# Delta rule of a hybrid layer on one core: inverse, solution, outputs and norms for two heads at once, with the projections in another order

## The chip, the cores and the metric

One core of one Trainium2 chip runs the whole program. The metric is device time in microseconds (us). An engine runs its own instructions in order; the five that matter here are called PE (TensorE's products), PEld (its loads of stationary operands, which run beside the products), DVE (VectorE), ACT (ScalarE) and POOL (GpSimd). SP issues the loads of the weights.

## The reference, cut to what matters

A sequence of 256 tokens with 1024 channels passes through two blocks. The first (two layers of attention and feed-forward) is not touched. The second is a hybrid layer: eight heads of a gated delta rule and four of a retention read the same projections, are gated and summed, and a feed-forward follows.

```
def chunk_gated_delta_rule(q, k, v, beta, g):       # 8 heads, d_k 128, d_v 256, chunks of 64 tokens
    ...
    lower = jnp.where(strict, jnp.einsum('bhncd,bhnmd->bhncm', k_beta, k) * decay, 0.0)
    t_inv = lax.linalg.triangular_solve(lower, eye, left_side=True, lower=True, unit_diagonal=True)
    u = jnp.einsum('bhncm,bhnme->bhnce', t_inv, v * beta[..., None])
    w = jnp.einsum('bhncm,bhnmd->bhncd', t_inv, k_beta * jnp.exp(g_cum)[..., None])
    attn = jnp.where(causal, jnp.einsum('bhncd,bhnmd->bhncm', q, k) * decay, 0.0)
    ...                                             # a scan over the chunks with a state
...
qkv = jax.nn.silu(causal_depthwise_conv(jnp.concatenate([qa, ka, va], axis=-1), conv_a))
oa = chunk_gated_delta_rule(qa, ka, va, beta, g)
oa = rmsnorm_2(oa, norm_a) * jax.nn.silu(za)
```

The kernel solves the same triangular system in two blocks of 128 tokens for each head: it inverts each 128x128 unit triangular block, solves the first, carries it over to the second, solves that, and multiplies by the masked q k matrix.

## The kernel before, in words

**Main work and pieces.** All large products run as three products of a high and a low part in fp32r (`hi`, `lo` for the weights, `XH`/`XL` or `OH`/`OL` for the activations). The weights come in chunks of 1024 rows by 256 columns; a chunk is four pieces, and a piece of the kind met here is 12 products with a 128x128 stationary operand and 256 columns. DVE and ACT split each weight into `hi` (line 188) and `lo` (line 197) ahead of its use.

**Side work, a step at a time.** All else is written as generators. The emission loop (lines 1600 to 1612) issues one piece of products, then lets each active generator run up to its next `yield`, in the order in which they were started, and then issues loads and splits of weights to come. So the order on every engine is fixed when the program is built: a `yield` puts one piece of main products between two steps, and PE stands still only where the next instruction in its order isn't ready.

**A head of the delta rule** (`delta_task`, line 1046) takes q and k from the chunk `wqka`, convolves them (`conv_silu`), and nine pieces later forms the two product groups k k and q k (line 1064, four products). DVE then makes the norms (1069 to 1075), scales with decay and beta into `nLT` and `AT` (1076, 1078), puts the small diagonal blocks in place (1082) and transposes them (1083). Then come twelve steps of an inverse that doubles its blocks (1088 to 1139): in each step a group of small products (32x32 up to s = 5, 64x64 at s = 6) and a copy by ACT (`X`) or by DVE (`DD`, `DT`) that the next step's products need. After it come three products of 256 columns with pauses between them (1146, 1150, 1155: the solution in `z` and `w`), the outputs (1164, 1165), sums for the norm (1176), a power by POOL (1179), and the scaling and split into `OH`, `OL`. A product of plain fp32 is two instructions on PE.

**The order of the chunks** is q and k of head h, v of h, the gate z of h; so heads follow each other every 12 pieces, and steps of three heads fall between the same pieces. Tiles that live over several steps are held in rings (`RING`, line 261); a task that finds its ring full runs the other generators until a place is free.

**Banks.** Main products write to two banks `w` in turn (`wbank`, line 278; two of four banks `d` while results wait for a norm's factors), side work to two banks `s` and the four `d`. The gate's chunk of head 0 asks for a bank `d` by name (line 1225).

Of the kernel before, what the change touches and what calls it, by code (L numbers as in the profile page):

```python
# [30 lines left out]
# steps that side work lets pass before it needs what others make for it  # L31
# [34 lines left out]
def body(ctx: ExitStack, tc: tile.TileContext, a):  # L66
# [42 lines left out]
    # the gains first, then x; what is needed later comes behind the first weights  # L109
# [98 lines left out]
    def ahead(i):  # L208
        """what may be loaded and split once the products of piece i are issued"""
# [50 lines left out]
    # tiles that are held over steps: no more of them than the ring has  # L260
    RING = {"y": 2, "qk": 3, "qn": 2, "v": 4, "zg": 4, "DD": 3, "nLT": 3, "AT": 3, "z": 2}

    def hold(shape, tag):
# [3 lines left out]
        if tag == "z":  # L267
            zn[0] += 1
            return REG[:, 3072 + 512 * (zn[0] % 2):3584 + 512 * (zn[0] % 2)].rearrange("p (a b) -> p a b", a=2)
        return TW(shape, tag, RING[tag])  # L270

    zn = [0]
# [15 lines left out]
    wn = [0]  # L288
# [23 lines left out]
    def products(todo, xl_last=False):  # L312
        """(out, hi, lo, xh, xl, first, last): what was split last comes last"""
# [33 lines left out]
    def N_chunk(src, xs, n, post):  # L347
        """n < 128 columns in a piece"""
# [41 lines left out]
    def D_tail(grp, src, n, ops, post, pre=None):  # L390
        """the last two chunks, a bank after the other"""
# [18 lines left out]
    def W_pair(src, xs, posts):  # L410
        """two chunks of outputs at once, over the tiles of x"""
# [23 lines left out]
    def X_pair(src, xs, posts):  # L435
        """512 columns, a bank for each half of the tokens"""
# [29 lines left out]
    def split(src, hi, lo):  # L466
        """the second part a step after the first"""
# [25 lines left out]
    def sum_ch(out, parts):  # L493
        """sums over the channels, a token per partition; 32 tokens at a time, as the weights' load is what they take"""
# [19 lines left out]
    def renorm():  # L514
        """the splits of x * g * r, for the chunks after the first"""
# [73 lines left out]
    # over the keys of two blocks, for the queries of the second: all of the first, or with the window  # L589
# [4 lines left out]
    # key > query: column > partition  # L594
# [16 lines left out]
    def attend(q, k, v, slot, window=False, sink=None, delay=0, done=False):  # L611
        """q, k: [128, T], a head on each half of the partitions; v(t, half) -> [128, 64]"""
# [38 lines left out]
        for h in range(2):  # L651
# [3 lines left out]
            # blocks: (q0, k0), (q1, k0), (q1, k1)  # L655
# [11 lines left out]
    # ================= the first block =================  # L667
# [7 lines left out]
    def feed_x(b, g, xs, norm, norm2=None, g2=None, first=False):  # L675
        """after xT's pair b is complete: x * g and its splits, the squares"""
# [31 lines left out]
    # attention of layer 0  # L708
# [59 lines left out]
    def tables():  # L768
        """of the second block"""
# [9 lines left out]
    # feed-forward with a short convolution  # L779
# [63 lines left out]
    # attention of layer 1  # L843
# [45 lines left out]
    # ================= between the blocks =================  # L889
# [7 lines left out]
    def stat2():  # L897
# [4 lines left out]
        # r1 = 1 / sqrt(mean x^2 + eps), and r1 r2 with r2 the factor of x g r1  # L902
# [23 lines left out]
    # ================= the second block =================  # L926
# [10 lines left out]
    def decay_task(bank):  # L937
        # beta and g, a token per partition
# [63 lines left out]
    def conv4(src, u, y, base):  # L1002
        """src, u, y: [128, 2, T]; tiles base[i] of conv_a"""
# [37 lines left out]
    # the small blocks on the diagonal, and the transposes of the inverses  # L1041
    BLOCKS = [slice(o, o + 32) for o in range(0, 128, 32)]
    FULL = [(T1([128, 2, 128], name="DT%d" % i), T1([64, 2, 64], name="DF%d" % i)) for i in range(3)]
    ident32 = T1([128, 32], name="ident32")

    def delta_task(h, bank):
# [3 lines left out]
        q, k = qk[:, 0], qk[:, 1]  # L1050
        sq = TW([128, 512], "sq")[:, :T]
        S.activation(sq, q, AF.Square)
        # the norms of k go into beta and v, those of q into the norm behind
        tk, bk, nbk = (TW([128, 2], n, 1) for n in ("tk", "bk", "nbk"))
        qe, kv = (TW([128, 2], n, 3) for n in ("qe", "kv"))
        # the inverse, block by block of twice the size: D (0) and its transpose (1)
        DD = hold([128, 2, 2, 32], "DD")
        DT, DF = FULL[h % 3]
        V.tensor_copy(DD[:, 1], bc(ident32, 2))
        nLT, AT = hold([128, 384], "nLT"), hold([128, 384], "AT")  # L1060
        nd = nLT.rearrange("p (b c) -> p b c", b=3)[:, 0:3:2]
        for x, out, b in ((k, nLT, nbk), (q, AT, bk)):
# [24 lines left out]
        V.tensor_scalar(qe, p[:, 0:2], 128.0 * EPS, 128.0 * EPS * EPS, op0=OP.mult, op1=OP.add)  # L1087
        for s in range(1, 7):
            yield
            p = PT()  # L1090
            pv = p[:, :128].rearrange("p (b c) -> p b c", b=2)
            pd = p[:, :64].rearrange("p (b c) -> p b c", b=2)
            X = TW([128, 2, 64], "X")
            Xd = X.rearrange("p b c -> p (b c)")[:, :64].rearrange("p (b c) -> p b c", b=2)
            if s < 5:
                for o in BLOCKS:
                    for b in range(2):
                        mm(pd[o, b], nd[o, b, o], DD[o, 0, b], True, True)
                cp("S", Xd, pd)
            elif s == 5:  # L1100
                for o in (0, 64):
                    for b in range(2):
                        mm(pd[o + 32:o + 64, b], nd[o:o + 32, b, o + 32:o + 64], DD[o:o + 32, 0, b], True, True)
                for o in (32, 96):
                    cp("S", Xd[o:o + 32], pd[o:o + 32])
            else:
                for b in range(2):
                    mm(pv[64:128, b], nd[0:64, b, 64:128], DF[:, b], True, True)
# [3 lines left out]
            pv = p[:, :128].rearrange("p (b c) -> p b c", b=2)  # L1112
            pd = p[:, :64].rearrange("p (b c) -> p b c", b=2)
            if s < 5:
                for o in BLOCKS:
                    for b in range(2):
                        mm(pd[o, b], DD[o, 1, b], Xd[o, b], True, True)
            elif s == 5:
                for o in (32, 96):
                    for b in range(2):  # L1120
                        mm(pd[o:o + 32, b], DT[o:o + 32, b, o:o + 32], Xd[o:o + 32, b], True, True)
            else:
                for b in range(2):
                    mm(pv[0:64, b], X[64:128, b], DT[64:128, b, 64:128], True, True)
            if s < 5:
                V.copy_predicated(DD[:, 0], bc(lvl[:, s], 2), pd)
# [7 lines left out]
            elif s == 5:  # L1134
                V.tensor_copy(DF[32:64, :, 0:32], pd[32:64])
                V.transpose(DT[0:32, :, 32:64], pd[32:64])
                V.transpose(DT[64:96, :, 96:128], pd[96:128])
            else:
                V.tensor_copy(DT[0:64, :, 64:128], pv[0:64])
        while h not in vt:  # L1140
            yield
        v = vt.pop(h)
        z = hold([128, 2, 256], "z")
# [6 lines left out]
        mm(p[:, :256], nLT[:, 128:256], z[:, 0], True, True)  # L1150
        w = TW([128, 256], "e")
        V.tensor_tensor(w, v[:, 1], p[:, :256], op=OP.add)
        yield
        p = PT()
        mm(p[:, :256], DT[:, 1], w, True, True)
        cp("S", z[:, 1], p[:, :256])
        free("v", "DD", "nLT")
        while h not in sz:
            yield
        yield  # L1160
        p = PT()
        for e in range(2):
            c = slice(e * 128, e * 128 + 128)
            mm(p[:, e * T:e * T + T], z[:, 0, c], AT[:, 0:256], True, False)
            mm(p[:, e * T + 128:e * T + T], z[:, 1, c], AT[:, 256:384], False, True)
        free("z", "AT")
        sq = square(p)
        zg = sz.pop(h)
        for e in range(2):
            if e:  # L1170
# [599 lines left out]
```

## Time and profile before

| what | value |
|---|---|
| three runs | 1344.65, 1344.09, 1341.1 us (median 1344.09) |
| span of the profiled execution | 1341.2 us (its time beyond the span is not listed) |
| PE busy | 1317.4 us, 98% |
| PEld, DVE, ACT, POOL busy | 93%, 73%, 55%, 2% |
| instructions on PE | 11824 |
| granted TensorE clock | 0.995 of full speed over the span |
| HBM read | 212.86 MB, 159 GB/s |

The stage of the delta rule lies between about 605 and 876 us of the span. A busy PE is not PE at its peak; what a group of instructions costs PE is read from the start of its first load of a stationary operand to the start of the next group's first load.

### The profile page before, as it was taken

The page shows a single profiled execution, that of the slowest core. Times are in us where ns is not written, and L with a number is a line of the kernel's source. Part 1 is how long each engine was busy: PE and PEld are TensorE (multiplying, and loading weights), DVE is VectorE, ACT ScalarE, POOL GpSimd, SP SyncE. Part 2 cuts the span into 40 slices and gives each one's busy share as a digit, 9 for nine tenths or more (in the row PEclk, how much of TensorE's full clock was granted, in tenths as well). Part 3 has the DMA queues.
Part 4 walks back from the last instruction along what each step waited for, and adds up shares of the span by engine and source line. Part 5 has one row for each costly group of instructions (what it writes and reads, how often), then busy time and mean ns, then how long its engine had stood idle before and what let it go on. Part 6 is the DMA issues. An engine that isn't in the chain of part 4 may idle for free.

```text
span 1341.2 us, 29103 instructions
## 1 busy us (share of the span) xinstructions
PE 1317.4 (98%) x11824; PEld 1250.3 (93%) x11824; DVE 984.4 (73%) x2225; ACT 731.6 (55%) x1202; POOL 27.2 (2%) x38
## 2 busy tenths in 40 slices
PE   7999999999999999999999999999999999999998
PEld 6999999998889999999888888999999999999996
DVE  6997887778878877788778888666557556855554
ACT  6665765555765655566545544444343445655553
POOL 0000000000000000000000000000000000000000
PEclk9999999998999999999999999999999999999999
DMA  7435565554334655544333333445455564465652
GB/s 240 156 127 183 175 205 188 186 181 142 107 117 156 215 189 189 185 133 158 115 107 114 110 126 104 134 157 191 150 179 168 173 196 153 160 219 184 189 183 89
DMA packets 60470, 215.79 MB, mean 161 GB/s; under 512 B 6832, under 2 KB 7600, under 8 KB 60336
## 3 DMA queue, kind: packets, MB, share of 16 engines
q1 hardware_dynamic: 59328, 212.31, 49.1%
q8 instruction: 93, 1.52, 0.5%
q10 hardware_dynamic: 1008, 1.63, 0.4%
q14 instruction: 41, 0.34, 0.1%
HBM read 212.86 MB, written 1.05 MB: 159 GB/s over the span
## 4 chain that ended last, share of the span: by engine, by line
PE 92%; DVE 4%; ACT 2%; issue 1%; DMA 1%; POOL 0%; SPq 0%; POOLq 0%; DVEq 0%; ACTq 0%
PE ps_w L134 54%; PE ps_d L134 33%; PE ps_s L134 4%; PE ps_s L145 1%; ACT h L634 1%; DVE lo L197 1%; PE ps_d L145 1%; DMA xT<-in_x 0%; DMA raw<-in_wv0p 0%; DVE y L794 0%; ACT hi L188 0%; DVE XL L464 0%; DVE h L626 0%; DVE y L1369 0%; DVE DD L1082 0%
## 5 line engine op out<-in xcount | busy, mean ns | idle before, releaser
L197 DVE TENSOR_TENSOR lo<-raw,hi 128x512 fp32r<-128x512 f32 x801 | 519.7, 684 | 93.5 <-ACT hi L188 92.7
L188 ACT ACTIVATE hi<-raw 128x1024 fp32r<-128x1024 f32 (+1 forms) x403 | 418.1, 1046 | 168.9 <-PE ps_w L134 85.7
L134 PE MATMUL ps_w<-XH,hi 128*128 128x256 f32 x976 | 168.3, 295 | 2.5 <-ACT XH L1454 1.4
L134 PE MATMUL ps_w<-XL,hi 128*128 128x256 f32 x976 | 156.3, 283 | 0.0
L134 PE MATMUL ps_w<-XH,lo 128*128 128x256 f32 x976 | 156.1, 282 | 0.0
L134 PE MATMUL ps_w<-OH,hi 128*128 128x256 f32 x896 | 144.8, 284 | 0.0
L134 PE MATMUL ps_w<-OH,lo 128*128 128x256 f32 x896 | 142.9, 282 | 0.3 <-DVE lo L197 0.3
L134 PE MATMUL ps_w<-OL,hi 128*128 128x256 f32 x896 | 142.5, 281 | 0.0
L134 PEld LDWEIGHTS ps_w<-XH,hi 128*128 128x128 f32 x976 | 134.4, 191 | 7.8 <-ACT XH L1454 1.7
L134 PEld LDWEIGHTS ps_w<-XL,hi 128*128 128x128 f32 x976 | 133.8, 190 | 0.0
L134 PEld LDWEIGHTS ps_w<-XH,lo 128*128 128x128 f32 x976 | 133.6, 190 | 0.0
L134 PE MATMUL ps_d<-OH,hi 128*128 128x256 f32 x776 | 126.0, 283 | 0.0
L134 PEld LDWEIGHTS ps_w<-OH,hi 128*128 128x128 f32 x896 | 121.5, 188 | 3.6 <-issue 3.5
L134 PE MATMUL ps_d<-OL,hi 128*128 128x256 f32 x776 | 124.4, 281 | 0.0
L134 PE MATMUL ps_d<-OH,lo 128*128 128x256 f32 x776 | 124.3, 281 | 0.0
L134 PEld LDWEIGHTS ps_w<-OH,lo 128*128 128x128 f32 x896 | 122.1, 189 | 0.5 <-DVE lo L197 0.5
L134 PEld LDWEIGHTS ps_w<-OL,hi 128*128 128x128 f32 x896 | 121.7, 188 | 0.0
L134 PEld LDWEIGHTS ps_d<-OH,hi 128*128 128x128 f32 x776 | 104.9, 188 | 1.9 <-issue 1.7
L134 PEld LDWEIGHTS ps_d<-OL,hi 128*128 128x128 f32 x776 | 105.1, 187 | 0.3 <-DVE OL L470 0.2
L134 PEld LDWEIGHTS ps_d<-OH,lo 128*128 128x128 f32 x776 | 105.1, 188 | 0.2
L790 ACT ACTIVATE y<-u,prm 128x256 f32<-128x256 f32 x88 | 48.0, 595 | 62.4 <-DVE u L764 62.4
L764 DVE TENSOR_TENSOR u<-ps_w,RB 128x512 f32<-128x512 f32 x44 | 30.1, 689 | 63.0 <-PE ps_w L134 56.8
(378 smaller groups left out, 1644.7 us busy)
## 6 DMA issues: line engine op xcount, KB each, us to landing
raw<-in_wu SPq DMA_DIRECT2D x108, 512.0 KB, 4.2
raw<-in_wd SPq DMA_DIRECT2D x68, 512.0 KB, 3.9
raw<-in_wgb SPq DMA_DIRECT2D x24, 512.0 KB, 3.7
raw<-in_wqk SPq DMA_DIRECT2D x16, 512.0 KB, 4.0
raw<-in_wza SPq DMA_DIRECT2D x16, 512.0 KB, 3.8
raw<-in_wqkb SPq DMA_DIRECT2D x16, 512.0 KB, 4.1
raw<-in_wbra SPq DMA_DIRECT2D x16, 512.0 KB, 4.2
raw<-in_wbrb SPq DMA_DIRECT2D x16, 512.0 KB, 4.7
```

The source lines that it names most:

```text
L134: PE.matmul(out, lhsT, rhs, start=start, stop=stop, skip_group_check=True)
L145: PE.transpose(out, in_, ident)
L188: S.activation(hi[:, :w], raws[n][:, :w], AF.Copy)
L197: V.tensor_tensor(lo[:, c], raws[n][:, c], hi[:, c].bitcast(F32), op=OP.subtract)
L634: S.activation(e[h][:, c], e[h][:, c], AF.Exp, bias=nm[:, i:i + 1], accum_out=sums[:, i:i + 1])
L764: V.tensor_tensor(u, v2(bank), bc(RB, 2), op=OP.mult)
L790: S.activation(y[:, i], u[:, i], AF.Identity, bias=P_(cb, t), scale=P_(cw, 3 * t + 2))
```

## The change

Two heads form a pair. Each head still has its own convolution, its own k k and q k groups, and its own rows of `nLT` and `AT`. From there `pair_task`, which the second head of the pair enters, does the transposes, all twelve steps of the inverse, the solution and the norm for both heads: tiles have a dimension for the head, a step issues the products of both heads one behind the other, and one copy serves both. The products are the same in number and shape. The outputs of the two heads come in two steps, one behind the other. The chunks of a pair now come in the order q k (even head), z (even), q k (odd), v (even), z (odd), v (odd); the first pair starts with q k and v of head 0 together, as before. `wbank` no longer counts: it gives `w` while fewer than two results wait for a norm, else `d`, with room for six that wait; the gate of head 0 takes its bank from it. The rings of `DD`, `nLT` and `AT` hold two pairs, that of `z` one. A group of `d` chunks first lets waiting results go. Comments go, and the reserve for descriptors of dynamic transfers is set to 1024.

```
-    RING = {"y": 2, "qk": 3, "qn": 2, "v": 4, "zg": 4, "DD": 3, "nLT": 3, "AT": 3, "z": 2}
+    RING = {"y": 2, "qk": 3, "qn": 2, "v": 4, "zg": 4, "DD": 2, "nLT": 2, "AT": 2, "z": 1}
...
     def wbank(more=0):
-        if len(deferred) >= 4:
+        if len(deferred) + more >= 6:
             drain(cur["stat"])
-            late(1)
-        wn[0] += 1
-        if len(deferred) + more >= 2 and wn[0] % 4 in (3, 0):
-            return PT("d")
-        return PT("w")
+            late()
+        return PT("w" if len(deferred) + more < 2 else "d")
...
             if c == 0:
                 if s == 0:
+                    if deferred:
+                        drain(cur["stat"])
+                        late()
...
     def delta_task(h, bank):
...
+        q, k, i = qk[:, 0], qk[:, 1], h % 2
+        if i == 0:
+            P = pairs[h // 2] = Pair()
+            P.DD = hold([128, 2, 4, 32], "DD")
+            P.nLT, P.AT = hold([128, 2, 384], "nLT"), hold([128, 2, 384], "AT")
+            P.DT, P.DF = FULL[h // 2 % 2]
...
-        for x, out, b in ((k, nLT, nbk), (q, AT, bk)):
+        for x, out, b in ((k, P.nLT[:, i], nbk), (q, P.AT[:, i], bk)):
...
             if x is k:
                 for o in BLOCKS:
-                    V.copy_predicated(DD[o, 1], bc(lvl[o, 0], 2), nd[o, :, o])
-                V.transpose(DD[:, 0], DD[:, 1])
+                    V.copy_predicated(P.DD[o, 1, 2 * i:2 * i + 2], bc(lvl[o, 0], 2), nd[o, :, o])
         free("qk")
+        if i:
+            yield from pair_task(h // 2, P)
+
+    def pair_task(n, P):
+        DD, DT, DF, nLT, AT = P.DD, P.DT, P.DF, P.nLT, P.AT
+        heads = (2 * n, 2 * n + 1)
+        V.transpose(DD[:, 0], DD[:, 1])
         p = PT()
-        sum_ch(p, [sq])
+        for i in range(2):
+            sum_ch(p[:, 2 * i:2 * i + 2], [P.sq[:, i]])
...
         for s in range(1, 7):
             yield
...
                 for o in BLOCKS:
-                    for b in range(2):
-                        mm(pd[o, b], nd[o, b, o], DD[o, 0, b], True, True)
+                    for g in range(4):
+                        mm(pd[o, g], nd(g)[o, o], DD[o, 0, g], True, True)
                 cp("S", Xd, pd)
...
             yield
...
-                V.copy_predicated(DD[:, 0], bc(lvl[:, s], 2), pd)
+                V.copy_predicated(DD[:, 0], bc(lvl[:, s], 4), pd)
                 if s < 4:
                     V.transpose(DD[:, 1], DD[:, 0])
...
-        mm(p[:, :256], DT[:, 0], v[:, 0], True, True)
-        cp("S", z[:, 0], p[:, :256])
+        for i in range(2):
+            mm(p[:, i * T:i * T + T], DT[:, 2 * i], v[i][:, 0], True, True)
+        cp("S", z[:, :, 0], v2(p))
...
-            W_chunk(a["wva"][h - 1], xs0, va_post(h))
-        W_chunk(a["wza"][h], xs0, z_post(h), None, "d" if h == 0 else None)
+        if h % 2 == 0:
+            W_chunk(a["wza"][h], xs0, z_post(h))
+        else:
+            if h > 1:
+                W_chunk(a["wva"][h - 2], xs0, va_post(h - 1))
+            W_chunk(a["wza"][h], xs0, z_post(h))
+            W_chunk(a["wva"][h - 1], xs0, va_post(h))
...
-    nc = bacc.Bacc("TRN2", target_bir_lowering=False, num_devices=1)
+    nc = bacc.Bacc("TRN2", target_bir_lowering=False, num_devices=1, dynamic_dma_scratch_size=1024)
```

## Rows read from the trace of the kernel before

**Rows 1.** The page: span, and busy time of the engines.
```profile
span 1341.2 us, 29103 instructions
PE 1317.4 (98%) x11824; PEld 1250.3 (93%) x11824; DVE 984.4 (73%) x2225; ACT 731.6 (55%) x1202; POOL 27.2 (2%) x38
```
**Rows 2.** Windows: one period of a head (length, then busy time by engine).
```profile
749.15:777.28 28.13, 28.09 (x358) 24.95 (x357) 22.76 (x67) 14.21 (x29) 1.77 (x2) 1.00 0.37 114
```
**Rows 3.** Chain that ended last: start, length, what; a feed-forward stage, a norm's sums.
```profile
461.67 11.36 PE ps_w L134 x96
...
600.71 1.63 PE ps_s L134 x96
```
**Rows 4.** Timeline of PEld in the same period: start, busy time, operation, tiles, count.
```profile
749.86 0.27 PEld L134 LDWEIGHTS ps_s<-DD,nLT 32*32 32x32 f32 x16 [0.41 <-PE ps_d L134]
750.17 0.54 PEld L134 LDWEIGHTS ps_w<-XH,hi 128*128 128x128 f32 x4
...
751.78 0.24 PEld L134 LDWEIGHTS ps_d<-X,DD 32*32 32x32 f32 x16
752.06 0.53 PEld L134 LDWEIGHTS ps_w<-XH,hi 128*128 128x128 f32 x4
...
753.47 0.30 PEld L134 LDWEIGHTS ps_d<-REG,nLT 128*128 128x128 f32 x2
754.11 0.24 PEld L134 LDWEIGHTS ps_d<-DD,nLT 32*32 32x32 f32 x16 [0.33 <-DVE lo L197]
...
758.50 1.40 PEld L134 LDWEIGHTS ps_d<-AT,REG 128*128 128x128 f32 x8
760.02 0.23 PEld L134 LDWEIGHTS ps_d<-DD,nLT 32*32 32x32 f32 x16
...
767.82 0.21 PEld L134 LDWEIGHTS ps_d<-DD,nLT 32*32 32x32 f32 x8
768.07 0.54 PEld L134 LDWEIGHTS ps_w<-XH,hi 128*128 128x128 f32 x4
...
771.55 0.30 PEld L134 LDWEIGHTS ps_d<-DF,nLT 64*64 64x64 f32 x4
771.92 0.54 PEld L134 LDWEIGHTS ps_w<-XH,hi 128*128 128x128 f32 x4
...
773.90 0.73 PEld L134 LDWEIGHTS ps_d<-qk 128*128 128x128 f32 x4
...
775.41 0.22 PEld L134 LDWEIGHTS ps_d<-ones,sq 128*32 128x32 f32 x16
775.64 0.53 PEld L134 LDWEIGHTS ps_w<-XH,hi 128*128 128x128 f32 x4
```
**Rows 5.** Timeline of PEld behind the last head, where no inverse runs.
```profile
864.52 0.31 PEld L134 LDWEIGHTS ps_d<-REG,nLT 128*128 128x128 f32 x2
864.85 0.64 PEld L134 LDWEIGHTS ps_w<-XH,hi 128*128 128x128 f32 x4
...
866.36 0.31 PEld L134 LDWEIGHTS ps_d<-e,DT 128*128 128x128 f32 x2
```
**Rows 6.** Timeline of DVE behind the k k and q k groups at 773.90.
```profile
776.65 0.94 DVE L1082 COPY_PREDICATED DD<-lvl,nLT 32x64 f32<-32x64 uint8 x4
777.63 0.24 DVE L1083 STREAM_TRANSPOSE DD<-DD 128x64 f32<-128x64 f32 x1
777.80 0.44 DVE L1076 SCALAR_TENSOR_TENSOR AT<-ps_s,bk,REG 128x256 f32<-128x256 f32 x1
778.16 0.34 DVE L1078 SCALAR_TENSOR_TENSOR AT<-ps_s,bk,REG 128x128 f32<-128x128 f32 x1
```
**Rows 7.** Timeline of DVE behind the small products at 751.78.
```profile
752.94 0.22 DVE L1126 COPY_PREDICATED DD<-lvl,ps_d 128x64 f32<-128x64 uint8 x1
```
**Rows 8.** Timeline where the gate's chunk of head 0 starts.
```profile
622.33 0.73 PE L134 MATMUL ps_d<-XH,hi 128*128 128x256 f32 x4
...
623.41 1.28 DVE L764 TENSOR_TENSOR u<-ps_w,RB 128x512 f32<-128x512 f32 x2
```

More of the change, by code (lines that the diff above doesn't have):

```diff
@@ L1042, in body @@
     BLOCKS = [slice(o, o + 32) for o in range(0, 128, 32)]
-    FULL = [(T1([128, 2, 128], name="DT%d" % i), T1([64, 2, 64], name="DF%d" % i)) for i in range(3)]
+    FULL = [(T1([128, 4, 128], name="DT%d" % i), T1([64, 4, 64], name="DF%d" % i)) for i in range(2)]
     ident32 = T1([128, 32], name="ident32")
+    class Pair:
+        pass
+    pairs = {}
     def delta_task(h, bank):
@@ L1049, in delta_task @@
         yield from pause(2)
-        q, k = qk[:, 0], qk[:, 1]
-        sq = TW([128, 512], "sq")[:, :T]
-        S.activation(sq, q, AF.Square)
-        tk, bk, nbk = (TW([128, 2], n, 1) for n in ("tk", "bk", "nbk"))
[L1055 to L1061, printed above, removed]
-        for x, out, b in ((k, nLT, nbk), (q, AT, bk)):
+        q, k, i = qk[:, 0], qk[:, 1], h % 2
[4 more added lines that the diff above has]
+            P.DT, P.DF = FULL[h // 2 % 2]
+            P.sq, P.qe = TW([128, 2, T], "sqq", 1), TW([128, 4], "qe", 2)
+            V.tensor_copy(P.DD[:, 1], bc(ident32, 4))
+        P = pairs[h // 2]
+        S.activation(P.sq[:, i], q, AF.Square)
+        tk, bk, nbk = (TW([128, 2], n, 1) for n in ("tk", "bk", "nbk"))
+        kv = TW([128, 2], "kv", 4)
+        nd = P.nLT[:, i].rearrange("p (b c) -> p b c", b=3)[:, 0:3:2]
+        for x, out, b in ((k, P.nLT[:, i], nbk), (q, P.AT[:, i], bk)):
             p = PT()
@@ L1101, in delta_task @@
                 for o in (0, 64):
-                    for b in range(2):
-                        mm(pd[o + 32:o + 64, b], nd[o:o + 32, b, o + 32:o + 64], DD[o:o + 32, 0, b], True, True)
+                    for g in range(4):
+                        mm(pd[o + 32:o + 64, g], nd(g)[o:o + 32, o + 32:o + 64], DD[o:o + 32, 0, g], True, True)
                 for o in (32, 96):
@@ L1106, in delta_task @@
             else:
-                for b in range(2):
-                    mm(pv[64:128, b], nd[0:64, b, 64:128], DF[:, b], True, True)
+                for g in range(4):
+                    mm(pv[64:128, g], nd(g)[0:64, 64:128], DF[:, g], True, True)
                 cp("S", X[64:128], pv[64:128])
@@ L1111, in delta_task @@
             p = PT()
-            pv = p[:, :128].rearrange("p (b c) -> p b c", b=2)
-            pd = p[:, :64].rearrange("p (b c) -> p b c", b=2)
+            pv = p[:, :256].rearrange("p (b c) -> p b c", b=4)
+            pd = p[:, :128].rearrange("p (b c) -> p b c", b=4)
             if s < 5:
                 for o in BLOCKS:
[L1116 to L1125, printed above, removed]
-                V.copy_predicated(DD[:, 0], bc(lvl[:, s], 2), pd)
+                    for g in range(4):
+                        mm(pd[o, g], DD[o, 1, g], Xd[o, g], True, True)
+                V.copy_predicated(DD[:, 0], bc(lvl[:, s], 4), pd)
                 if s < 4:
@@ L1134, in delta_task @@
             elif s == 5:
+                for o in (32, 96):
+                    for g in range(4):
+                        mm(pd[o:o + 32, g], DT[o:o + 32, g, o:o + 32], Xd[o:o + 32, g], True, True)
                 V.tensor_copy(DF[32:64, :, 0:32], pd[32:64])
@@ L1138, in delta_task @@
             else:
+                for g in range(4):
+                    mm(pv[0:64, g], X[64:128, g], DT[64:128, g, 64:128], True, True)
                 V.tensor_copy(DT[0:64, :, 64:128], pv[0:64])
-        while h not in vt:
+        while any(h not in vt for h in heads):
             yield
-        v = vt.pop(h)
-        z = hold([128, 2, 256], "z")
+        v = [vt.pop(h) for h in heads]
+        z = hold([128, 2, 2, 256], "z")
         yield
         p = PT()
-        mm(p[:, :256], DT[:, 0], v[:, 0], True, True)
@@ L1147, in delta_task @@
-        cp("S", z[:, 0], p[:, :256])
+        for i in range(2):
+            mm(p[:, i * T:i * T + T], DT[:, 2 * i], v[i][:, 0], True, True)
+        cp("S", z[:, :, 0], v2(p))
         yield from pause(2)
         p = PT()
-        mm(p[:, :256], nLT[:, 128:256], z[:, 0], True, True)
-        w = TW([128, 256], "e")
-        V.tensor_tensor(w, v[:, 1], p[:, :256], op=OP.add)
+        w = TW([128, 2, T], "w", 1)
+        for i in range(2):
+            mm(p[:, i * T:i * T + T], nLT[:, i, 128:256], z[:, i, 0], True, True)
+            V.tensor_tensor(w[:, i], v[i][:, 1], p[:, i * T:i * T + T], op=OP.add)
@@ L1153, in delta_task @@
         yield
         p = PT()
[L1155 to L1158, printed above, removed]
-            yield
[L1160 to L1165, printed above, removed]
-        free("z", "AT")
-        sq = square(p)
@@ L1168, in delta_task @@
-        zg = sz.pop(h)
-        for e in range(2):
-            if e:
-                V.tensor_tensor(sq[:, :T], sq[:, :T], sq[:, T:], op=OP.add)
-            V.scalar_tensor_tensor(zg[:, e], p[:, e * T:e * T + T], P_("norm_a", e), zg[:, e],
-                                   op0=OP.mult, op1=OP.mult)
+        for i in range(2):
+            mm(p[:, i * T:i * T + T], DT[:, 2 * i + 1], w[:, i], True, True)
+        cp("S", z[:, :, 1], v2(p))
+        free("v", "v", "DD", "nLT")
+        while any(h not in sz for h in heads):
+            yield
@@ new lines, in pair_task @@
+        zg, sqs = [sz.pop(h) for h in heads], []
+        for i in range(2):
+            yield
+            p = PT()
+            for e in range(2):
+                c = slice(e * 128, e * 128 + 128)
+                mm(p[:, e * T:e * T + T], z[:, i, 0, c], AT[:, i, 0:256], True, False)
+                mm(p[:, e * T + 128:e * T + T], z[:, i, 1, c], AT[:, i, 256:384], False, True)
+            sq = square(p)
+            sqs.append(sq)
+            for e in range(2):
+                if e:
+                    V.tensor_tensor(sq[:, :T], sq[:, :T], sq[:, T:], op=OP.add)
+                V.scalar_tensor_tensor(zg[i][:, e], p[:, e * T:e * T + T], P_("norm_a", e), zg[i][:, e],
+                                       op0=OP.mult, op1=OP.mult)
@@ L1174, in delta_task @@
+        free("z", "AT")
         yield from pause(2)
         p = PT()
-        sum_ch(p, [sq[:, :T]])
-        tok, rt = TW([128, 2], "tok2", 4), TW([128, 2], "rt2", 4)
-        V.scalar_tensor_tensor(tok[:, :2], p[:, :2], 1.0 / 256, qe, op0=OP.mult, op1=OP.add)
-        G.tensor_tensor(rt[:, :2], tok[:, :2], mhalf[:, :2], op=OP.pow)
+        for i in range(2):
+            sum_ch(p[:, 2 * i:2 * i + 2], [sqs[i][:, :T]])
+        tok, rt = TW([128, 4], "tok4", 2), TW([128, 4], "rt4", 2)
+        V.scalar_tensor_tensor(tok, p[:, :4], 1.0 / 256, P.qe, op0=OP.mult, op1=OP.add)
@@ L1180, in delta_task @@
+        G.tensor_tensor(rt, tok, mhalf[:, :4], op=OP.pow)
         yield from pause(6)
         p = PT()
-        rows(rt, 2, p)
-        V.tensor_tensor(zg, zg, bc(p[:, :T], 2), op=OP.mult)
-        yield
-        yield from split(zg, OH[:, 2 * h:2 * h + 2], OL[:, 2 * h:2 * h + 2])
-        free("zg")
+        rows(rt, 4, p)
+        for i in range(2):
+            V.tensor_tensor(zg[i], zg[i], bc(p[:, i * T:i * T + T], 2), op=OP.mult)
+        for i, h in enumerate(heads):
+            yield
+            yield from split(zg[i], OH[:, 2 * h:2 * h + 2], OL[:, 2 * h:2 * h + 2])
+            free("zg")
```

17 lines of the change are left out of this document (8 added, 9 removed).

## The prediction

> **What bounds the kernel now.** I read the page first: PE is busy for 1317.4 of 1341.2 us, no other engine for more than three quarters [rows 1]. A busy PE says little by itself, so the question for the stage of the delta rule is what PE is busy with. The windows view gives one period of a head: 28.13 us, in which PE is never idle and DVE works for 22.76 us, 81% [rows 2]. The period holds 12 pieces of main products. What a piece costs by itself is read in the chain, in a feed-forward stage: 96 products in 11.36 us, so 12 in 1.42 us [rows 3]. 12 pieces are 17.04 us; the other 11.1 us of each period are side work on PE, in PE's own order. The change can give time back only out of these 11.1 us, or lose it by new waits of PE.
>
> The timeline of PEld shows where they go, group by group, start to start [rows 4]. A group of 16 small products takes 0.28 us (751.78 to 752.06), one of 8 0.25 us (767.82 to 768.07), four of 64x64 0.37 us (771.55 to 771.92). Beside that, a change of shape costs by itself: the piece ahead of a small group takes 1.61 us (750.17 to 751.78) and not 1.42, so 0.19 for letting the full-size products run out. A product of 256 columns in front of a small group takes 0.64 us (753.47 to 754.11), while behind the last head, where a piece follows, it takes 0.33 us (864.52 to 864.85) and delays the next piece by 0.09 us (864.85 to 866.36 is 1.51) [rows 5]. So side work is dear by its number of groups and changes of shape more than by its products.
>
> **The change part by part.** All prices are per pair, two periods of 28.13 us now, 24 pieces before and after.
>
> The joined inverse. Now: twice 8 groups of 16, 2 of 8 and 2 of 64x64, 2 x (8 x 0.28 + 2 x 0.25 + 2 x 0.37) = 6.96 us. After: 8 groups of 32, 2 of 16, 2 of eight 64x64. What the further products of a group cost no row shows directly. Below: 8 to 16 products cost 0.03 us more, 4 ns each [rows 4]. Above: 96 sums with 32 columns take 1.63 us, 17 ns each [rows 3]. Four products in a row will now use the same corner of the array, where the 8 to 16 step only filled other corners, so I go nearer to the upper end: 12 ns, 0.19 us for 16, 0.10 for 8. For four more of 64x64 I take 0.22 us, between 0.05 (four at 12 ns) and another 0.37. Sum after: 8 x 0.47 + 2 x 0.35 + 2 x 0.59 = 5.64 us. Gain 1.32 us (from -0.1 with 17 ns and 0.37, to 2.6 with 4 ns and 0.05).
>
> The Trainium skill (TensorE: Matmul & The Clock Gate, section "Wait — 56ns, not 53.3ns?") states that starts of matmuls never follow closer than about 25 ns, however small. By it 16 more would cost 0.40 us, and the joined inverse 8 x 0.68 + 2 x 0.45 + 2 x 0.59 = 7.5 us, more than now. The row speaks against it: 16 in 0.28 us is 17.5 ns each with the change of shape in it.
>
> Changes of shape. Now eight pieces of a period stand in front of small groups (seven of the inverse, one of the norm's sums): 16 x 0.19 = 3.04 us per pair. After, by the counts of yields, the inverse has twelve pieces of 24 in front of it and the norm one: 13 x 0.19 = 2.47 us. Gain 0.57 us.
>
> The products around it. Six products of 256 columns per pair stand in front of small groups now: 6 x 0.64 = 3.84 us. After, the second head enters the pair nine pieces behind its chunk, at piece 21 of the 24; the inverse takes pieces 22 to 33, which is 9 of the next pair; the solution falls on 11, 13 and 14, the outputs on 15 and 16, the sums on 18. So no inverse runs beside them: 6 x 0.33 + 2 x 0.09 = 2.16 us. The outputs (1.52 us, 758.50 to 760.02, an inverse step behind them [rows 4]) lose the same 0.19: gain 0.38. Together 2.06 us. The k k and q k groups, transposes, sums and rows of factors stay as they are in number; I cost them at nothing.
>
> The new wait at the join. Now DVE transposes the blocks (777.63, 0.24 us) before it makes `AT` [rows 6]. After, the transposes stand in `pair_task`, behind both `AT` instructions, and the inverse's first products wait for them. From the start of k k at 773.90 [rows 4] DVE ends the block copies at 777.59, +3.69; `AT` takes 0.70 (777.80 to 778.50); the transposes of twice the width take 0.31 (between 0.24 and 0.49); 0.1 to hand over: +4.80. PE has by then k k and q k with one head's sums (773.90 to 775.64, 1.74), the other head's sums 0.23, and a piece, 1.61: +3.58. Nothing else stands there in the new order, where now the rows and the first product of the solution of the head before do. PE waits 1.2 us per pair, and behind it all main products, since they are in PE's queue. If DVE comes late, as at 752.94, 1.16 us behind the start of a group that takes 0.28 [rows 7], the wait is 2.1; it can't be under 1.1, as `AT` stays.
>
> The gate's chunk of head 0. It has a bank of its own now and starts at 622.33; the bank that it would get by the new `wbank` is that of q k of head 0, which DVE reads until 623.41 + 0.64 = 624.05 [rows 8]. PE waits 1.7 us, once (nothing, if DVE came earlier). Elsewhere `wbank` gives what it gave: where two results wait, the old count had fallen on `d` as well.
>
> Order, rings, other engines. By the yields a gate tile of a pair is free at piece 52 of its count and the chunk that needs the place ends at 56, so the ring of four `zg` holds; v, y and q k rings have a place over too. The weights only change their order in SP's queue, with the same bytes. DVE and ACT save short instructions (of 45.5 us of DVE per pair [rows 2] some 3, an estimate: half of about 26 like the transposes of 0.24 [rows 6]); as neither bounds the stage I cost that at nothing, and it matters only if the cover goes: DVE would then have 42 us of work in some 53. Reserve and `d` groups: nothing, no results wait there.
>
> **Sum.** Per pair 1.32 + 0.57 + 2.06 - 1.2 = 2.75 us, four pairs 11.0, less 1.7 at the gate: 9.3 us. The last head's three products already stand free [rows 5], which takes 0.9 off, and the first heads' own waits of today give about as much back; I leave both out. The span goes from 1341.2 to 1331.9 us. The runs shown have a median of 1344.09, 2.9 above that span; a run after it should take 1344.09 - 9.3 = 1334.8 us. Own range: all low ends (wait 2.1, inverse at -0.1) leave 0 us, but both together are unlikely, so 1340; high ends (4 ns, no wait at the gate) 15 us, 1329.
>
> **The rivals.** *Groups add up.* If a product of a joined group costs as much as one does now, shape and all (17.5 ns in a group of 16), the twelve joined groups cost the old 6.96 us and only the changes of shape and the free products are saved: 9.3 - 4 x 1.32 = 4.0 us, 1340.1. For it: four in a row on one corner; against: 8 to 16 costs 0.03 us. The Trainium skill's 25 ns (the section above) would take another 4 x 0.5 us off, 1342.
>
> *No wait at the join.* If a step of another head falls in the gap, the 1.2 us are covered: 14.1 us, 1330.0. Against it: the counts of yields leave pieces 21 and 22 without other work.
>
> *DVE sets the pace of the inverse (slower).* Each step's products need a copy or transposes that DVE does behind the products of the step before. Now other heads' work lies between many of these; after, a step is a piece and a group, 1.61 + 0.47 = 2.08 us. DVE needs about 0.44 us until it sees a group, 0.6 for a wide copy and transposes, 0.1 and the longer group 0.2: some 1.35, so 0.7 us are spare, about one split of weights. At 752.94 DVE was 0.7 us late already [rows 7]. It turns the result once 24 such steps wait over 0.39 us each on the mean, that is, once DVE is late by 1.1 us throughout; with two splits in front of each, waits of 0.7 us, 24 x 0.7 = 16.8 us are lost: 1344.09 + 7.5 = 1351.6. Against it: 81% load now, and less work in it after.
>
> *It does not come about.* If tasks run into full rings, the generators run without pieces between them and PE waits for chains instead; some 9 us of it leave no change, 1344.
>
> **How the numbers follow.** What a measurement of this kernel can tell from no change is about 0.3%, 4.0 us: the runs lie 3.6 us apart. Chances: my forecast 0.60, groups add 0.12, no wait 0.08, DVE 0.09, no effect 0.11. Faster than 1340.1: nearly all of the first, half of the second, the third: 0.71. Within 0.3%: the rest of these and the last: 0.20. Slower: 0.09. The range from 1328 to 1343 holds the first three and a part of the last.
>
> **What would show it right or wrong.** Right: a pair's window of some 53.5 us where two heads take 56.3; groups of 32 small products at about 0.47 us; products of the solution with pieces on both sides at 0.33; a wait of PE of about 1.2 us for the transposes, four times; one of about 1.7 us near 622. Wrong: groups of 32 at 0.56 or more; gaps in front of most steps of the inverse with DVE named; bursts of side work without pieces, at the gate chunks above all.

## The result, and the profile after

| | before | after |
|---|---|---|
| runs, us (median) | 1341.1 to 1344.65 (1343.77), five | 1348.74 to 1357.03 (1351.24), five |
| span of the profiled execution, us | 1341.2 | 1355.2 (its time 1356.98) |
| its granted clock | 0.995 | 0.989 |

The ratio is 1.0069, with an interval of 1.0045 to 1.0093: the change costs some 7.5 us. The forecast was 1334.8 and its range ended at 1343; both were wrong, and so was the sign.

The page of after answers to [rows 1]:

```profile
span 1355.2 us, 28944 instructions
PE 1322.8 (98%) x11824; PEld 1265.1 (93%) x11824; DVE 975.2 (72%) x2149; ACT 724.7 (53%) x1158; POOL 25.2 (2%) x32
```

PE issues exactly as many products as before, and DVE and ACT have less to do. PEld is busy 14.8 us longer with the same 11824 loads: the products have become dearer, not more (a part of it lies in the stretches at a lower clock, below). The timeline of PEld, in the first pair's inverse and solution, shows which ones (to be read against [rows 4] and [rows 5]):

```profile
660.49 0.78 PEld L134 LDWEIGHTS ps_d<-DD,nLT 32*32 32x32 f32 x32 [1.39 <-DVE DD L1093]
661.31 0.54 PEld L134 LDWEIGHTS ps_w<-XH,hi 128*128 128x128 f32 x4
...
665.37 0.78 PEld L134 LDWEIGHTS ps_d<-DD,nLT 32*32 32x32 f32 x32
666.20 0.53 PEld L134 LDWEIGHTS ps_w<-XH,hi 128*128 128x128 f32 x4
...
667.81 0.78 PEld L134 LDWEIGHTS ps_s<-X,DD 32*32 32x32 f32 x32
...
680.38 0.48 PEld L134 LDWEIGHTS ps_s<-DD,nLT 32*32 32x32 f32 x16
680.90 0.54 PEld L134 LDWEIGHTS ps_w<-XH,hi 128*128 128x128 f32 x4
...
684.63 0.54 PEld L134 LDWEIGHTS ps_d<-DF,nLT 64*64 64x64 f32 x8
685.24 0.54 PEld L134 LDWEIGHTS ps_w<-XH,hi 128*128 128x128 f32 x4
...
690.18 0.74 PEld L134 LDWEIGHTS ps_s<-v,DT 128*128 128x128 f32 x4
690.94 0.64 PEld L134 LDWEIGHTS ps_w<-XH,hi 128*128 128x128 f32 x4
...
693.88 0.31 PEld L134 LDWEIGHTS ps_d<-REG,nLT 128*128 128x128 f32 x2
695.66 0.30 PEld L134 LDWEIGHTS ps_d<-REG,nLT 128*128 128x128 f32 x2 [1.47 <-DVE w L1164]
695.99 0.65 PEld L134 LDWEIGHTS ps_w<-XH,hi 128*128 128x128 f32 x4
```

A group of 32 takes 0.82 us, start to start (660.49 to 661.31; 0.83 from 665.37 to 666.20), where two groups of 16 took 2 x 0.28. At `s == 5` 16 products over two corners take 0.52 (680.38 to 680.90), where 16 over four corners took 0.28 before. The eight of 64x64 take 0.61. `v,DT` is four records in 0.76, as cheap as forecast. The first block step's `REG,nLT`, though, needs 2.11 us (693.88 to 695.99), because the second head's product starts 1.47 us late.

The chain of waits, PE alone, 600 to 900 us of after: engine, tile and line that waited, what it waited for, us in total, times, longest.

```profile
PE ps_d L134 <- DVE DD L1093: 5.3, 4, 1.4
PE ps_d L134 <- DVE w L1164: 2.6, 4, 1.1
PE ps_w L134 <- ACT hi L188: 1.7, 1, 1.7
```

The first is the forecast wait at the join, the third stands at 621, where the forecast put the gate's bank. The second was in no part of the forecast.

DVE at the join of the second pair answers to [rows 6]: the block copies (L1085), both `AT` instructions (L1079, L1081), then the transposes of `pair_task` (L1093), which end at 712.00; PE's group starts at 712.11.

```profile
710.07 0.93 DVE L1085 COPY_PREDICATED DD<-lvl,nLT 32x64 f32<-32x64 uint8 x4
711.04 0.48 DVE L1079 SCALAR_TENSOR_TENSOR AT<-ps_d,bk,REG 128x256 f32<-128x256 f32 x1
711.44 0.34 DVE L1081 SCALAR_TENSOR_TENSOR AT<-ps_d,bk,REG 128x128 f32<-128x128 f32 x1
711.70 0.30 DVE L1093 STREAM_TRANSPOSE DD<-DD 128x128 f32<-128x128 f32 x1
```

Last, three windows of after: the period of a pair (from one group of `ones,sqq` to the next), and two stretches in which the granted clock was the lower level, 1.2 GHz. Columns as in [rows 2]; the third number from the end is the clock.

```profile
770.47:830.90 60.43, 58.54 (x713) 54.66 (x713) 43.29 (x115) 26.45 (x47) 2.71 (x3) 0.94 0.33 108
714.12:724.36 10.24, 10.24 (x125) 9.44 (x123) 1.79 (x4) 3.11 (x6) 0.00 (x0) 0.50 0.33 104
775.56:782.39 6.83, 6.83 (x70) 6.21 (x71) 1.85 (x5) 0.98 (x2) 0.00 (x0) 0.50 0.48 154
```

The pair takes 60.43 us, 6.83 of them at 1.2 GHz; two heads took 56.26 [rows 2]. Before each of the two stretches PE had stood at the join and had then run a group of 0.82 us. The profile of before has no such stretch in this stage. The five runs of after fall into two kinds: spans of 1355.2 at a clock of 0.989 twice, 1347.0 to 1348.4 at 0.995 to 0.996 three times. The loss of clock costs the first kind some 7 us, an estimate from the two kinds of span; the others are still slower than before without it.

### The profile page after: what moved, and what is told of

Its sections match the earlier page's. It is cut to its first block, busy times and chain, and to the rows that moved or that the text cites. A ratio compares the mean times of both kernels' runs of the same rounds, so it can differ in the third digit from the quotient of the medians.

```text
span 1355.2 us, 28944 instructions
## 1 busy us (share of the span) xinstructions
PE 1322.8 (98%) x11824; PEld 1265.1 (93%) x11824; DVE 975.2 (72%) x2149; ACT 724.7 (53%) x1158; POOL 25.2 (2%) x32
## 4 chain that ended last, share of the span: by engine, by line
PE 90%; DVE 5%; ACT 2%; issue 1%; DMA 0%; POOL 0%; SPq 0%; POOLq 0%; DVEq 0%; ACTq 0%
PE ps_w L134 52%; PE ps_d L134 32%; PE ps_s L134 4%; DVE lo L197 1%; PE ps_s L145 1%; PE ps_d L145 1%; ACT h L629 1%; DMA xT<-in_x 0%; ACT hi L188 0%; DVE y L789 0%; DVE DD L1085 0%; DVE OL L686 0%; DVE XL L459 0%; DVE y L1392 0%; DVE h L621 0%
## 5 line engine op out<-in xcount | busy, mean ns | idle before, releaser
L134 PE MATMUL ps_w<-XH,lo 128*128 128x256 f32 x992 | 160.5, 285 | 0.0
L134 PE MATMUL ps_w<-XL,hi 128*128 128x256 f32 x992 | 160.0, 284 | 0.0
L134 PEld LDWEIGHTS ps_w<-XH,hi 128*128 128x128 f32 x992 | 138.2, 192 | 8.6 <-ACT hi L188 3.3
L134 PEld LDWEIGHTS ps_w<-XH,lo 128*128 128x128 f32 x992 | 137.6, 192 | 0.0
L134 PEld LDWEIGHTS ps_w<-XL,hi 128*128 128x128 f32 x992 | 137.0, 192 | 0.0
```

Source lines behind the costliest of these rows:

```text
L134: PE.matmul(out, lhsT, rhs, start=start, stop=stop, skip_group_check=True)
```

## The experiments

All edits are made on the kernel after, unless said. The expectation printed with each was written before its run. Beside the first four the runs of before had a median of 1343.51 us, beside the last four 1343.58.

**The order of the small products.** A call of `mm` with f32 operands leaves two records, so a group of 32 records is 16 calls. The kernel after issues four calls in a row on one 32x32 corner of the array (`for o ... for g`); before issued two. This edit turns the loops round, so that each call goes to another corner than the one ahead of it. Number and shapes of products, banks and what DVE reads are the same.

```
-                for o in BLOCKS:
-                    for g in range(4):
+                for g in range(4):
+                    for o in BLOCKS:
                         mm(pd[o, g], nd(g)[o, o], DD[o, 0, g], True, True)
...
-                for o in (32, 96):
-                    for g in range(4):
+                for g in range(4):
+                    for o in (32, 96):
```

> The changed kernel, with the small products of a joined group issued so that neighbours lie on different corners of the array (head and block outside, corner inside) up to s = 5. Theory 'one corner': products on one corner follow each other at about 30 ns, as their starts in the changed kernel's trace do, and PE overlaps corners only where they come close behind each other in its order. Then a group of 32 falls from 0.82 us to 0.36-0.45 (eight instructions of a corner at 30 ns and 0.12 to run out), one of 16 at s = 5 from 0.52 to about 0.38; per pair 8 x 0.4 + 2 x 0.14 = 3.5 us, 14 us in all, 1351.2 to about 1337. Rival 'floor': a small product costs some 25 ns in PE's order wherever it lies (0.82 us over 32 is 25.6 ns); then the groups stay at 0.8 us and the time at 1351. This floor is what the Trainium skill (TensorE: Matmul & The Clock Gate, section "Wait — 56ns, not 53.3ns?") states.

Measured: 1334.95 us (1333.2 to 1336.55), ratio 0.9937 [0.9922, 0.9952] against before: 16.3 us less than after, by an order of loops. Its timeline of PEld:

```profile
661.74 0.34 PEld L134 LDWEIGHTS ps_d<-DD,nLT 32*32 32x32 f32 x32 [1.40 <-DVE DD L1093]
662.12 0.54 PEld L134 LDWEIGHTS ps_w<-XH,hi 128*128 128x128 f32 x4
...
678.10 0.33 PEld L134 LDWEIGHTS ps_s<-DD,nLT 32*32 32x32 f32 x16
678.47 0.54 PEld L134 LDWEIGHTS ps_w<-XH,hi 128*128 128x128 f32 x4
```

The group of 32 takes 0.38 us and that of 16 on two corners 0.37. So a floor under the distance of two starts is not what made it 0.82: 0.38 / 32 is 12 ns a record, with the change of shape in it. The timeline of PE over the first 0.15 us of such a group, after first (665.37:665.52) and then this kernel (665.73:665.88), shows 4 records started and 16:

```profile
665.37 0.31 PE L134 MATMUL ps_d<-DD,nLT 32*32 32x32 f32 x4
...
665.73 0.33 PE L134 MATMUL ps_d<-DD,nLT 32*32 32x32 f32 x16
```

Read record by record, the same two groups show what the order changes. In both, the eight records of one corner start at 0, 53, 84, 116, 148, 179, 211 and 243 ns, counted from the corner's first: behind the second they are 32 ns apart. In this kernel the four corners do that at the same time, their first records at 0, 7, 14 and 20 ns. In after the corners' first records start at 0, 153, 307 and 460 ns, so the last record of the group starts at 703 ns and not at 263: that is the whole difference of 0.44 us. (Which record is on which corner is taken from the order of the program; each of the four series has the same steps.) In before, with four records in a row on a corner, the next corner started after 14 ns. In both cases three records of the corner ahead were still to start.

The period of a pair (columns as above) falls to 53.80 us, at full clock throughout:

```profile
760.02:813.82 53.80, 51.91 (x713) 48.30 (x713) 43.22 (x115) 26.51 (x47) 2.72 (x3) 1.00 0.37 121
```

The waits at the join (5.3 us) and for `w` (2.6) stand there as in after.

**Two calls in a row.** Two runs over the corners for `s < 5`, with two calls on each corner, as before did it; `s == 5` stays as in after.

```
-                for o in BLOCKS:
-                    for g in range(4):
+                for e in (0, 2):
+                    for o in BLOCKS:
+                        for g in (e, e + 1):
```

> The changed kernel, with each group of 32 issued as two runs over the four corners, two products of a corner in a row in each, which is how the kernel before issued 16; s = 5 stays. Theory 'one corner': two runs of about 0.16 us and 0.12 to run out, 0.44 us instead of 0.82; 8 x 0.38 x 4 = 12 us, about 1339. Rival 'floor': 0.8 us, 1351. If PE's view ahead is too short even for this, something between.

Measured: 1338.54 us (1335.35 to 1339.05), ratio 0.9966 [0.9952, 0.998]. Groups of 32 take 0.42 us, while at `s == 5`, still four in a row, 16 cost 0.52:

```profile
660.20 0.38 PEld L134 LDWEIGHTS ps_d<-DD,nLT 32*32 32x32 f32 x32 [1.41 <-DVE DD L1093]
660.62 0.53 PEld L134 LDWEIGHTS ps_w<-XH,hi 128*128 128x128 f32 x4
...
676.83 0.48 PEld L134 LDWEIGHTS ps_s<-DD,nLT 32*32 32x32 f32 x16
677.35 0.53 PEld L134 LDWEIGHTS ps_w<-XH,hi 128*128 128x128 f32 x4
```

One, two and four calls in a row on a corner: 0.38, 0.42 and 0.82 us. A second costs 0.04 us, the third and fourth another 0.40.

**The transposes ahead of `AT`.** Each head's transposes go into its own step, behind the block copies of `k`; the one in `pair_task` goes away.

```
+                V.transpose(P.DD[:, 0, 2 * i:2 * i + 2], P.DD[:, 1, 2 * i:2 * i + 2])
...
-        V.transpose(DD[:, 0], DD[:, 1])
```

> The changed kernel, with the transposes of the block starts (DD) done for each head behind its block copies, ahead of AT, as in the kernel before; nothing else. Theory: the wait of PE in front of the first group of the inverse (a piece of 3.03 us in place of 1.61, 1.42 us, four times) is DVE's AT and the transposes behind it: it falls to about 0.5 us (blocks copied at +3.69 us, transposed at +3.95, PE there at +3.58), 3.7 us in all, about 1347.5. Rival: DVE is late with other work; then the wait stays over 1 us and the time at 1351.

Measured: 1345.72 us (1343.51 to 1349.25), ratio 1.0018 [1.0005, 1.003]. PE's waits, 640 to 900 us (columns as above):

```profile
PE ps_d L134 <- DVE w L1164: 2.8, 4, 1.2
PE ps_d L134 <- DVE DD L1086: 1.3, 4, 0.4
```

The wait at the join falls from 5.3 to 1.3 us in all. 4 us of it were `AT` ahead of the transposes, as the forecast had it; what is left, 0.3 us a pair on the mean, is still a wait for the transposes, now behind the block copies alone. The time is 5.5 us under that of after, whose runs lie 8.3 us apart. This profile, with groups of 0.82 us and without the long wait, has no stretch of 1.2 GHz in the stage.

**Both products ahead of the additions.** In the solution's first block step both heads' products write halves of one bank, and the first head's addition, which reads that bank, stood between them in the program.

```
         for i in range(2):
             mm(p[:, i * T:i * T + T], nLT[:, i, 128:256], z[:, i, 0], True, True)
+        for i in range(2):
             V.tensor_tensor(w[:, i], v[i][:, 1], p[:, i * T:i * T + T], op=OP.add)
```

> The changed kernel, with both products of the solution's middle step issued before the two additions that read their bank. Theory: the second product waits for the first addition's read of the same bank (group of 1.55 to 2.11 us for two products that need 0.66-0.76): it falls to 0.76 us in all four pairs, 0.8 to 1.4 us each, about 3.7 us, 1347.5. Rival: what is late is z from ACT, or another bank; then the group keeps its length.

Measured: 1350.31 us (1350.01 to 1350.7), ratio 1.0052 [1.0037, 1.0067]. The four records stand in one row of the timeline and take 0.77 us, and the wait for `w` is gone from the view:

```profile
696.50 0.74 PEld L134 LDWEIGHTS ps_d<-REG,nLT 128*128 128x128 f32 x4
```

```profile
PE ps_d L134 <- DVE DD L1093: 5.4, 4, 1.4
```

The time is only 0.9 us under that of after, which the runs can't tell from nothing: this kernel still has groups of 0.82 us, and all its four runs were granted a clock of 0.991 to 0.994. The rows show the gain, the time doesn't.

**The bank of the gate's first chunk.** `wbank` is overruled for head 0, as in before.

```
-            W_chunk(a["wza"][h], xs0, z_post(h))
+            W_chunk(a["wza"][h], xs0, z_post(h), None, "d" if h == 0 else None)
```

> The changed kernel, with a bank d by name for the gate's chunk of head 0, as in the kernel before. Theory: the wait of 1.9 us ahead of this chunk (2.03 us from the last small product to the first main one, 0.11 without a wait) goes, 1351.2 to about 1349.3; by the trace it is clear, by the time it is not, as the runs of the changed kernel lie 8 us apart. Rival: PE waits there for the split of the weights and not for the bank, and the gap stays.

Measured: 1351.82 us (1349.13 to 1355.26), ratio 1.0063 [1.0044, 1.0081]: by the time nothing. PE where the chunk starts, after first and then this kernel (its trace runs 2.9 us behind that of after here):

```profile
621.30 0.22 PE L134 MATMUL ps_d<-MW,identb 128*128 128x128 bf16 x1
...
623.25 0.71 PE L134 MATMUL ps_w<-XH,hi 128*128 128x256 f32 x4 [1.73 <-ACT hi L188]
```

```profile
624.21 0.22 PE L134 MATMUL ps_d<-MW,identb 128*128 128x128 bf16 x1
624.23 0.73 PE L134 MATMUL ps_d<-XH,hi 128*128 128x256 f32 x4
```

With another bank the 1.73 us are gone. The view named ACT's split `hi`, whose end happened to come last; ACT runs the same split at the same place here (624.99, after's 622.09 and 2.9), and PE doesn't wait for it. The bank was the cause.

**All four edits together.**

> The changed kernel with four edits at once: neighbours on different corners (as in the run with corners, 1334.95 us), transposes behind each head's block copies, both middle products ahead of the additions, and the bank of its own for the gate's chunk of head 0. Theory: the four costs lie at different places of PE's order and add up: from 1335 the wait at the join takes 3.7 us, the additions 4.1, the bank 1.9: 1325.3, ratio to the kernel before about 0.987. Rival: what one wait gives back the next takes, as DVE is at some 80%; then it stays above 1330.

Measured: 1326.1 us (1323.19 to 1327.75), ratio 0.9868 [0.9854, 0.9881]: faster than both kernels. A pair's period and all of PE's waits in the stage:

```profile
755.27:807.35 52.08, 51.76 (x713) 48.42 (x712) 43.04 (x116) 26.55 (x47) 2.71 (x3) 1.00 0.38 124
```

```profile
PE ps_s L134 <- DVE DD L1086: 0.9, 3, 0.3
PE ps_d L134 <- DVE DD L1086: 0.3, 1, 0.3
```

It gains 8.9 us on the kernel with the corners alone, where the rows of the other three edits give 4.0 (join), 2.6 to 3.7 (additions) and 1.7 to 1.9 (bank), 8.3 to 9.6 in all: the costs add up.

**The corners in the kernel before.** The same turn of loops there, for `s < 5`, with `b` outside: one call in a row and not two.

```
-                for o in BLOCKS:
-                    for b in range(2):
+                for b in range(2):
+                    for o in BLOCKS:
```

> The kernel before, heads one by one, with neighbours on different corners up to s = 4 (two products per corner and group, now in a row). Theory 'one corner': the groups of 16 already overlap their corners, two products of a corner in a row are within PE's view: 0.28 us falls to 0.25 at most, 64 groups, 0 to 2 us, within the noise of 1343.5. Rival: if the order within a group mattered at any length, 0.28 would fall to about 0.2 and the time by 5 us.

Measured: 1341.46 us (1339.73 to 1345.14), ratio 0.9987 [0.9977, 0.9997]. A group of 16 takes 0.26 us (759.65 to 759.91), where it took 0.28:

```profile
759.65 0.21 PEld L134 LDWEIGHTS ps_d<-X,DD 32*32 32x32 f32 x16
759.91 0.53 PEld L134 LDWEIGHTS ps_w<-XH,hi 128*128 128x128 f32 x4
```

64 such groups make 1.3 us; the time is 2.1 us less. So the gain of the best kernel is not the turn of loops by itself. Joining the heads is what makes the order matter, and what pays once the order is right.

**The order of the chunks alone.** Before, with the new order of the gates' and v's chunks, and nothing joined.

```
+        if h % 2 == 0:
+            W_chunk(a["wza"][h], xs0, z_post(h), None, "d" if h == 0 else None)
+        else:
+            if h > 1:
+                W_chunk(a["wva"][h - 2], xs0, va_post(h - 1))
+            W_chunk(a["wza"][h], xs0, z_post(h))
...
-        W_chunk(a["wza"][h], xs0, z_post(h), None, "d" if h == 0 else None)
```

> The kernel before, heads one by one, with the chunks of q, k, z and v in the new order and nothing else of the change. Theory: the order only shifts which steps fall behind which piece; groups and their lengths stay, the time is 1343.5 within 4 us. Rival: the order itself costs (a ring runs full, v comes too late for its head) or gains several us; then the trace shows side work without pieces between, or fewer pieces of 1.61 us.

Measured: 1344.71 us (1342.81 to 1348.05), ratio 1.0009 [1.0, 1.0018]: the order costs nothing that the runs can tell. The rows aren't the same, though. PE's waits for the transposes (L1083) in the stage, before first and then this kernel:

```profile
PE ps_d L134 <- DVE DD L1083: 1.5, 3, 1.0
```

```profile
PE ps_d L134 <- DVE DD L1083: 2.7, 6, 1.0
PE ps_s L134 <- DVE DD L1083: 2.0, 2, 1.0
```

With the new order PE waits for them eight times, 4.7 us in all (the profile is of the longest run, 1348.05 us), and with the old one three times. So a part of the wait at the join is likely to come with the order and not with the joining.

## Why the prediction was wrong

The step that failed is the price of the joined groups: "12 ns, 0.19 us for 16, 0.10 for 8", which made 0.47 us of a group of 32 and 0.35 of the 16 at `s == 5`. They took 0.82 and 0.52. Per pair the joined inverse costs 8 x 0.82 + 2 x 0.52 + 2 x 0.61 = 8.82 us and not 5.64; over four pairs 12.7 us, more than the whole forecast gain of 9.3. The step from 8 to 16 products, 4 ns each, was read as the price of filling other corners, and the text said that four in a row would now share one; but no row of before had four in a row, and the value was put inside 4 to 17 ns when the truth, 0.54 us for 16 more, is 34 ns each. The upper bound came from sums of another shape, and was no bound for this. Shown is that the order decides (0.38, 0.42, 0.82 with nothing else changed). The Trainium skill (TensorEngine Tiling (Array Packing), section "Key Properties") says that different tiles of the array can load weights and multiply in parallel; the 0.38 us of alternating corners agree with it, and it would have been the place to ask what the same tile does four times in a row. The records show the rest: on one corner a record follows the one ahead at 32 ns in either order, and with eight in a row the next corner starts only after 153 ns. Why it doesn't start sooner no run shows.

The rival *Groups add up* asked the right question, but at 17.5 ns a product it was too cheap as well, and its 1340 was far off. The Trainium skill's rule (TensorE: Matmul & The Clock Gate, section "Wait — 56ns, not 53.3ns?") of about 25 ns between starts gives 0.82 / 32 = 25.6 ns here, and looks confirmed. It isn't: the same 32 in another order take 12 ns each. The number agrees, the reason doesn't, and taking it as a floor would have hidden the remedy.

A second term was missing: `REG,nLT` was counted with the free products. It took 2.11 us once and 1.55 three times, where 0.77 stands without the wait, 3.7 us in all. The addition of head 0 reads the bank into which the product of head 1 has still to write; the product waits for the addition, and the addition for its turn on DVE. In after's first pair the product's loads were through at 694.19 (693.88 + 0.31), and DVE came to the addition at 695.20, behind `y` and a split of weights:

```profile
693.81 0.87 DVE L1004 SCALAR_TENSOR_TENSOR y<-u,prm,y 128x254 f32<-128x254 f32 x2
694.59 0.68 DVE L197 TENSOR_TENSOR lo<-raw,hi 128x512 fp32r<-128x512 f32 x1
695.20 0.41 DVE L1164 TENSOR_TENSOR w<-v,ps_d 128x256 f32<-128x256 f32 x1
```

Joining two heads in one bank made two independent steps into a chain through DVE.

The other terms, against the forecast:

- The wait at the join: 1.3 us a pair (5.3 in four) for 1.2. The mechanism, `AT` ahead of the transposes, is shown by the edit that turned them round (1.3 us left in all).
- The gate of head 0: 1.7 to 1.9 us for 1.7, shown by the bank's edit.
- The eight of 64x64: 0.61 us for 0.59. Pieces ahead of small groups: 1.61 and pieces elsewhere 1.41 to 1.52, as costed.
- The products around the inverse: `v,DT` and `w,DT` took 0.77 us for a pair's four records, 0.38 a head for 0.33 and a delay.
- *DVE sets the pace* has no row for it, though its 1351.6 lies beside the measured 1351.24; that is chance. PE's waits in after and the kernels made from it name no step of the inverse behind the first; loads of later steps stand 0.2 us for DVE twice in the kernel with the corners alone and twice in the one with all edits. *No wait at the join* fell with the wait. *It does not come about* fell with the period: pieces stand between the groups as the yields had it.

Added up: -9.3 + 12.7 + 3.7 + 0.5 (join) + 0.2 (gate) = +7.8 us; measured +7.5. The runs also differ by their clock, so an agreement to 0.3 us is luck; the terms are good to a microsecond or two. A pair's period at full clock is a second way to check them: 53.5 by the forecast, 3.2 more for the groups, 0.8 for `REG,nLT` and 0.1 at the join make 57.6. In after the middle pairs hold stretches of 1.2 GHz, but the second pair of the kernel with both products ahead of the additions ran at full clock and took 56.81, without the 0.8:

```profile
710.00:766.81 56.81, 55.42 (x713) 52.14 (x712) 43.02 (x115) 26.57 (x47) 3.13 (x4) 1.00 0.35 115
```

The rest of the change (rings, `d` groups, reserve) was not run by itself; the sum leaves no time for it beyond a microsecond or two.

Two bounds of the forecast's inverse don't come out of its own figures: with 17 ns and 0.37 the gain is 0.3 us a pair and not -0.1, with 4 ns and 0.05 it is 2.8 and not 2.6. Neither brings the range near the result.

That the turned loops give 1334.95, the time forecast for after, is luck too: their groups, at 0.38, are cheaper than the 0.47 of the forecast, which saves 2.6 us, and the wait for `w`, in no part of the forecast, takes 3.7 back.

The loss of clock adds to this in some runs. Three of the four profiles of kernels with groups of 0.82 us have stretches of 1.2 GHz in this stage (after, and those with only the additions or only the bank changed; the one with early transposes has none), and none of the six others has, though two of these stand 1.4 us at each join. Each of the five stretches in these three profiles begins 1.2 to 2.0 us behind the start of a join's group. So they were seen only where both stood together, the wait of 1.4 us and the long groups behind it, and then at 5 joins of 12. That the two together cause it is argued from one profile a kernel, not shown.

## What to carry to other kernels

Before small products of several heads are put in one group, look at which part of the array each one uses: in a group, let each product go to another corner than the one ahead of it; joining pays then, and costs when the loop over heads is the inner one. When results of two heads share a bank, issue both products before the first reader. And where a price is taken from rows of another order or shape, the range has to hold the case that it isn't like them.

## What the runs showed of the hardware that was not expected

- 32 records of 32x32 products cost 0.38, 0.42 or 0.82 us with one, two or four calls in a row on a corner; on two corners 16 cost 0.37 alternating and 0.52 with four in a row. On one corner the records start 32 ns apart in either order; with the corners in turn four start within 20 ns, with eight records in a row the next corner starts 153 ns after the one ahead.
- A product that writes another half of a bank than the one being read stood until DVE had read the first half (1.47 us on PEld in the first pair); with both products ahead of the reads it didn't. The trace shows the wait; whether the chip or only the order that the program keeps asks for it, no run shows.
- The granted clock fell to 1.2 GHz for 10.24 and 6.83 us in a stage where no wait of PE was longer than 1.7 us. It stayed up in the profiles with the same waits and groups of 0.38 or 0.42 us, and in the one with the same groups and waits of 0.4 us at the joins.
